# Forming one operand of the first stage on VectorE instead of by accumulating loads

## The chip, the cores and the metric

The kernel runs on one core of one Trainium2 chip. The metric is the time of one execution on the device in microseconds (us); the kernel before takes 1924.87 us (median of three runs, 1923.51 to 1925.85).

## The reference, cut to what matters

A two-layer decoder trunk on x of 1024 tokens by 1024 channels, in float32. Layer 0 begins with one wide projection of x, and this is the first stage of the kernel:

```
proj = x @ w_in                       # 1024 x 1024 by 1024 x (3*2048 + 8)
xm, o_pre, z, gts = split(proj, [E, 2*E, 3*E], axis=-1)      # E = 2048
```

From xm come a causal convolution and q, k and v of an mLSTM cell; o_pre and z gate its result; gts (8 columns) are the cell's input and forget gates. A layer norm, a gated embedding, a short-convolution layer and a second gated embedding follow.

## The kernel before, in words

All of it works on tiles of 128 partitions by 512 float32. x lies transposed: `raw_x[c, h]` is channel block c (0 to 7) of token half h (0 or 1). TensorE works on pairs: `split` (lines 86 to 94) makes of a tile a rounded part "hi" (a cast on ScalarE, L91) and the remainder "lo" (a subtraction on VectorE, L94), and `three` (L104, L105, L106) adds up hi by hi, hi by lo and lo by hi: three matmuls where one was. The third one needs the lo part of the weights.

The projection is a two-by-two block product done with seven block products instead of eight (class `Projection`). A group g is a pair of 128-column blocks of weights, with four weight tiles a11, a12 (first row) and a21, a22 (second row). Product (g, n) multiplies the n-th of a11, a12, s2, s1, s3, s4, a22, where the s are sums of weight tiles formed on VectorE (L118), by its partner n11, b21, t2, t1, n3, n22 or n4, which are four tiles each (k = 0 to 3) formed of x. Of these, in the code's signs:

- n3 = x(k, 1) - x(k+4, 1), t2 = x(k, 0) - n3: `moving_1`
- T1 = x(k, 1) - x(k, 0): `moving_t1n` and `moving_t1`
- n4 = x(k+4, 0) - t2: `moving_n4n` and `moving_n4`, formed by ScalarE (the negative, L123) and an accumulating load on POOL's queue (L135)

One product is 12 matmuls of 128 by 512. The first six groups go in two passes: products (0,0), (0,1), (1,0), ... (5,1) first, since they need token half 0 and the first weight rows alone, and then (0,2) to (0,6), (1,2) and so on. Weights are prepared three products ahead of their use.

The table `EARLY_OPERANDS` names, for each operand step, the product after which it is written in the code and how many k go with one product. The engines' streams are fixed when the program is built, and each engine works its stream in order. SP issues all plain loads in one queue of its own; each of them waits for the landing of the one eight places before it. POOL's queue carries the accumulating loads and the stores of results.

T1 is made in three steps before. After products 0 and 1 ScalarE writes -x(k, 0) into a new tile (L123, `moving_t1n`), POOL issues a load that adds x(k, 1) from HBM onto it (`add_on`, L135), and after products 7 and 8 the tile is split (`moving_t1`). `gpack`, whose gate weights VectorE turns into `wghl` after product 7 (`prepare_constants`), is loaded by SP behind the last tile of x. `cpack` holds the other constants.

Of the kernel before, what the change touches and what calls it, by code (L numbers as in the profile page):

```python
# [11 lines left out]
ALU = mybir.AluOpType  # L12

P = 128
HALF = 512
# [16 lines left out]
PACE = 0.85  # L32
STORE_AFTER = 8
GATES_AT = 32
EARLY_OPERANDS = (("t1n", 0, 2), ("t2", 1, 1), ("n22", 5, 2), ("n4n", 5, 2), ("n3", 6, 2), ("t1", 7, 2), ("n4", 10, 2), ("b12", 24, 1))
PLAN = {
    -10: [("head",)],
    -9: [("xc", 0)],
# [22 lines left out]
def trunk(ctx: ExitStack, tc: tile.TileContext, I, out: bass.AP):  # L61
# [9 lines left out]
    def slot(dt=F32):  # L71
        count[0] += 1
        return sl.tile([P, HALF], dt, tag="s", name=f"{part[0]}_{count[0]}")
# [14 lines left out]
    def split(src, hi_on, lo_on):  # L88
        hi, lo = slot(F32R), slot(F32R)
        if hi_on == "act":  # L90
            nc.scalar.copy(hi, src)  # L91
        else:
            nc.vector.tensor_copy(hi, src)
        (nc.vector if lo_on == "dve" else nc.gpsimd).tensor_tensor(  # L94
            out=lo, in0=src, in1=hi.bitcast(F32), op=ALU.subtract)
        return hi, lo

    def cols(j, n=P):
        return slice(j * n, (j + 1) * n)
# [16 lines left out]
    def combined(a, b, op):  # L116
        d = slot()
        nc.vector.tensor_tensor(out=d, in0=a, in1=b, op=op)  # L118
        return d

    def evacuated(src, scale=1.0):
        t = slot()
        nc.scalar.activation(t, src, AF.Copy, scale=scale)  # L123
        return t
# [8 lines left out]
    def add_on(dst, src):  # L133

        nc.gpsimd.dma_start(dst, src, accum_op=ALU.add)  # L135
# [311 lines left out]
    def operands():  # L447
        return {key: [None] * 4 for key in ("n11", "b21", "t2", "t1", "n3", "n22", "n4")}
# [7 lines left out]
    ops = operands()  # L456
    raw_x = {}

    def load_x(c, h):
        raw_x[c, h] = slot()  # L460
        nc.sync.dma_start(raw_x[c, h], I["xt"][cols(c), cols(h, HALF)])
# [39 lines left out]
    cell = Projection(groups, lambda i, j: WA[i, j], ops, cell_result, EARLY_A, LEAD_A)  # L501
# [35 lines left out]
    for k in range(4):  # L537
        load_x(k + 4, 1)
        load_x(k, 1)
        if k < 3:  # L540
            cell.fetch(k + 2, 1)
    nc.sync.dma_start(gpack, I["gpack"])
    nc.sync.dma_start(cpack, I["cpack"])

# [16 lines left out]
    b12 = [None] * 4  # L561

    def moving_1(k):
        n3 = combined(raw_x[k, 1], raw_x[k + 4, 1], ALU.subtract)
        raw_x["n3", k] = n3
        raw_x["t2", k] = combined(raw_x.pop((k, 0)), n3, ALU.subtract)
        ops["t2"][k] = split(raw_x["t2", k], "act", "dve")

    def moving_t1n(k):
        raw_x["t1", k] = evacuated(raw_x[k, 0], -1.0)  # L570
        add_on(raw_x["t1", k], I["xt"][cols(k), cols(1, HALF)])

    def moving_n4n(k):
        raw_x["n4", k] = evacuated(raw_x.pop(("t2", k)), -1.0)
        add_on(raw_x["n4", k], raw_x.pop((k + 4, 0)))

    def moving_t1(k):
        ops["t1"][k] = split(raw_x.pop(("t1", k)), "act", "dve")

    def moving_n3(k):  # L580
        ops["n3"][k] = split(raw_x.pop(("n3", k)), "act", "dve")
# [7 lines left out]
    def moving_b12(k):  # L589
        b12[k] = split(raw_x.pop((k, 1)), "act", "dve")  # L590

    moving = {"t1n": moving_t1n, "t2": moving_1, "n4n": moving_n4n, "t1": moving_t1, "n3": moving_n3,
              "n22": moving_n22, "n4": moving_n4, "b12": moving_b12}

    def transposed(blocks):
# [377 lines left out]
    early = {}  # L973
    for f, at, n in EARLY_OPERANDS:
        for k in range(4):
# [435 lines left out]
    ops = operands()  # L1411
# [218 lines left out]
def build(arrays):  # L1630
    import concourse.bacc as bacc

    nc = bacc.Bacc("TRN2", target_bir_lowering=False, num_devices=1)
    I = {k: nc.dram_tensor(k, v.shape, mybir.dt.from_np(v.dtype), kind="ExternalInput").ap()
         for k, v in arrays.items()}
    out = nc.dram_tensor("out", (DM, SEQ), F32, kind="ExternalOutput").ap()
    with tile.TileContext(nc) as tc:
        trunk(tc, I, out)
    return nc
# [9 lines left out]
```

## Time and profile before

| what | value |
|---|---|
| median of three runs | 1924.87 us |
| the profiled execution, own time | 1925.12 us |
| its span, first to last instruction | 1923.4 us |
| TensorE busy | 1896.8 us (99%) |
| VectorE busy | 1463.8 us (76%) |
| ScalarE busy | 937.8 us (49%) |
| mean granted TensorE clock | 0.997 |

Times below are us from the span's start. PE is TensorE, DVE is VectorE, ACT is ScalarE, SPq is SP's issuing of loads. In a row of the timeline the first number is the start, the second the length, and the bracket tells how long the engine had stood before it and what it waited for. Consecutive instructions of one engine overlap a little, so the distance of two starts, and not the length, is what one more instruction costs. Names with numbers left out ("in", "start", "xt") are those of tiles: "start" tiles are allocated ahead of the first product, "in" tiles behind it, "wa" are the weights and "xt" is x in HBM.

### The profile page before, as it was taken

How to read it: one execution, taken by the hardware profiler on the slowest of the kernel's cores; microseconds unless marked ns; L12 is line 12 of the kernel's file. 1: busy time of each engine (PE TensorE's matmuls, PEld its weight loads, DVE VectorE, ACT ScalarE, POOL GpSimd, SP SyncE). 2: the span in 40 equal slices, each digit the busy share in tenths (PEclk: the TensorE clock that was granted, in tenths of full speed). 3: DMA queues.
4: the chain of work that ended last, by engine and by line, in shares of the span. 5: the costliest groups of instructions: out<-in, count | busy, mean ns of one | idle time of the engine just before them, and what ended most of it. 6: DMA issues, size and time to landing. Idle time of an engine off the chain costs nothing.

```text
span 1923.4 us, 26056 instructions
## 1 busy us (share of the span) xinstructions
PE 1896.8 (99%) x8654; PEld 1563.6 (81%) x8654; DVE 1463.8 (76%) x2528; ACT 937.8 (49%) x1741; POOL 288.7 (15%) x344
## 2 busy tenths in 40 slices
PE   8999999999999999999999999999999999999998
PEld 6778888888888888787878888888888888888887
DVE  7888888778777777757977787878787877745657
ACT  7655554546656544455665433333333333454553
POOL 1112332222001000034301000000000000031420
PEclk9999999999999999999999999999999999999999
DMA  8247767686556584896135535545646355699435
GB/s 253 91 155 226 240 216 229 202 246 233 178 184 215 187 286 155 325 348 191 56 130 159 141 129 176 183 161 149 197 161 190 134 156 155 215 361 325 143 115 192
DMA packets 197400, 374.35 MB, mean 195 GB/s; under 512 B 22768, under 2 KB 27152, under 8 KB 197264
## 3 DMA queue, kind: packets, MB, share of 16 engines
q1 hardware_dynamic: 169008, 301.88, 45.5%
q0 software_dynamic: 28256, 70.80, 14.2%
q8 instruction: 68, 1.11, 0.2%
q14 instruction: 68, 0.56, 0.1%
HBM read 239.40 MB, written 115.36 MB: 184 GB/s over the span
## 4 chain that ended last, share of the span: by engine, by line
PE 86%; DVE 5%; DMA 3%; ACT 2%; issue 1%; POOL 1%; SPq 0%; DVEq 0%; POOLq 0%; ACTq 0%
PE Pb L106 11%; PE Pb L104 11%; PE Pb L105 11%; PE Pin L104 7%; PE Pin L106 7%; PE Pin L105 7%; PE Pat L104 3%; PE Pat L106 3%; PE Pat L105 3%; PE Poutb L105 3%; PE Poutb L104 3%; PE Poutb L106 3%; PE Pouta L105 2%; PE Pouta L106 2%; PE Pgb L104 2%; PE Pgb L106 2%
## 5 line engine op out<-in xcount | busy, mean ns | idle before, releaser
L104 PE MATMUL Pb<-ga,b 128*128 128x512 f32 x852 | 331.4, 389 | 0.0
L105 PE MATMUL Pb<-ga,b 128*128 128x512 f32 x852 | 331.4, 389 | 0.0
L106 PE MATMUL Pb<-ga,b 128*128 128x512 f32 x852 | 327.1, 389 | 0.0
L91 ACT CAST b<-b 128x512 fp32r<-128x512 f32 x265 | 152.5, 617 | 160.9 <-DVE b L118 158.6
L104 PE MATMUL Pin<-in,in 128*128 128x512 f32 x488 | 191.0, 391 | 2.4 <-ACT in L91 1.3
L105 PE MATMUL Pin<-in,in 128*128 128x512 f32 x488 | 190.0, 389 | 0.0
L94 DVE TENSOR_TENSOR b<-b,b 128x512 fp32r<-128x512 f32 x265 | 176.6, 687 | 17.0 <-ACT b L91 15.4
L106 PE MATMUL Pin<-in,in 128*128 128x512 f32 x488 | 189.0, 391 | 0.0
L106 PEld LDWEIGHTS Pb<-ga,b 128*128 128x128 f32 x852 | 159.9, 188 | 33.4 <-DVE b L94 0.2
L105 PEld LDWEIGHTS Pb<-ga,b 128*128 128x128 f32 x852 | 159.9, 188 | 33.3
L104 PEld LDWEIGHTS Pb<-ga,b 128*128 128x128 f32 x852 | 159.9, 188 | 33.1
L91 ACT CAST in<-in 128x512 fp32r<-128x512 f32 x175 | 105.5, 615 | 89.9 <-DVE in L118 78.4
L94 DVE TENSOR_TENSOR in<-in,in 128x512 fp32r<-128x512 f32 x175 | 118.6, 687 | 23.9 <-ACT in L91 23.2
L123 ACT ACTIVATE b<-Pb 128x512 f32<-128x512 f32 x96 | 57.4, 598 | 129.0 <-PE Pb L106 129.0
L104 PE MATMUL Pat<-at,at 128*128 128x512 f32 (+3 forms) x297 | 112.4, 379 | 0.9 <-ACT at L91 0.9
L118 DVE TENSOR_TENSOR b<-b,b 128x512 f32<-128x512 f32 x167 | 110.9, 687 | 1.0 <-issue 0.2
L106 PE MATMUL Pat<-at,at 128*128 128x512 f32 (+3 forms) x297 | 109.6, 372 | 1.2 <-DVE at L859 1.2
L104 PEld LDWEIGHTS Pin<-in,in 128*128 128x128 f32 x488 | 91.6, 188 | 23.4 <-ACT in L123 2.1
L105 PE MATMUL Pat<-at,at 128*128 128x512 f32 (+3 forms) x297 | 110.0, 371 | 0.0
L106 PEld LDWEIGHTS Pin<-in,in 128*128 128x128 f32 x488 | 91.6, 188 | 20.8 <-DVE in L94 1.7
L105 PEld LDWEIGHTS Pin<-in,in 128*128 128x128 f32 x488 | 91.6, 188 | 18.8
L94 DVE TENSOR_TENSOR outa<-outa,outa 128x512 fp32r<-128x512 f32 x108 | 77.0, 771 | 23.9 <-ACT outa L91 23.8
(424 smaller groups left out, 4230.5 us busy)
## 6 DMA issues: line engine op xcount, KB each, us to landing
b<-wb SPq DMA_DIRECT2D x122, 256.0 KB, 4.1
in<-wa SPq DMA_DIRECT2D x86, 256.0 KB, 4.1
xcdram<-in POOLq DMA_DIRECT2D x56, 256.0 KB, 4.6
ydram<-b SPq DMA_DIRECT2D x56, 256.0 KB, 2.1
gwdram<-b SPq DMA_DIRECT2D x56, 256.0 KB, 2.2
gb<-gwdram SPq DMA_DIRECT2D x56, 256.0 KB, 3.4
outa<-ydram SPq DMA_DIRECT2D x52, 256.0 KB, 5.4
outb<-ydram SPq DMA_DIRECT2D x49, 256.0 KB, 5.4
```

Source lines behind the costliest of these rows:

```text
L91: nc.scalar.copy(hi, src)
L94: (nc.vector if lo_on == "dve" else nc.gpsimd).tensor_tensor(out=lo, in0=src, in1=hi.bitcast(F32), op=ALU.subtract)
L104: mm(acc, lh, rh, start=first, stop=False, skip_group_check=onto)
L105: mm(acc, lh, rl, start=False, stop=False, skip_group_check=onto)
L106: mm(acc, ll, rh, start=False, stop=last, skip_group_check=onto)
L118: nc.vector.tensor_tensor(out=d, in0=a, in1=b, op=op)
L123: nc.scalar.activation(t, src, AF.Copy, scale=scale)
```

## The change

`moving_t1n` is gone, and with it four ScalarE instructions and four accumulating loads of 256 KB. x(k, 0) is kept until T1 is formed; `moving_t1`, at its old place after products 7 and 8, now subtracts the two tiles of x on VectorE (`combined`, L118) and splits the result. Two weight fetches are called ahead of the constants: the first weight row of group 5 and the second weight row of group 0.

```diff
-EARLY_OPERANDS = (("t1n", 0, 2), ("t2", 1, 1), ("n22", 5, 2), ("n4n", 5, 2), ("n3", 6, 2), ("t1", 7, 2), ("n4", 10, 2), ("b12", 24, 1))
+EARLY_OPERANDS = (("t2", 1, 1), ("n22", 5, 2), ("n4n", 5, 2), ("n3", 6, 2), ("t1", 7, 2), ("n4", 10, 2), ("b12", 24, 1))
...
         if k < 3:
             cell.fetch(k + 2, 1)
+    cell.fetch(5, 1)
+    cell.fetch(0, 2)
     nc.sync.dma_start(gpack, I["gpack"])
     nc.sync.dma_start(cpack, I["cpack"])
...
         raw_x["n3", k] = n3
-        raw_x["t2", k] = combined(raw_x.pop((k, 0)), n3, ALU.subtract)
+        raw_x["b11", k] = raw_x.pop((k, 0))
+        raw_x["t2", k] = combined(raw_x["b11", k], n3, ALU.subtract)
         ops["t2"][k] = split(raw_x["t2", k], "act", "dve")
-
-    def moving_t1n(k):
-        raw_x["t1", k] = evacuated(raw_x[k, 0], -1.0)
-        add_on(raw_x["t1", k], I["xt"][cols(k), cols(1, HALF)])
...
     def moving_t1(k):
-        ops["t1"][k] = split(raw_x.pop(("t1", k)), "act", "dve")
+        ops["t1"][k] = split(combined(raw_x[k, 1], raw_x.pop(("b11", k)), ALU.subtract), "act", "dve")
```

Nowhere else does an engine's stream change. On VectorE, from the lo part of T1 for k = 0 (in_454<-in_219 before) to the lo part of the weight sum s2 of product (0,2) and the sums behind it, the stream before reads:

```order
L94 TENSOR_TENSOR in_454<-in_219,in_453 128x512
L94 TENSOR_TENSOR in_458<-in_222,in_457 128x512
L94 TENSOR_TENSOR in_466<-in_340,in_465 128x512
L424 TENSOR_TENSOR in_482<-Pin_504,in_482 128x512
L94 TENSOR_TENSOR in_485<-in_243,in_484 128x512
L94 TENSOR_TENSOR in_489<-in_246,in_488 128x512
L118 TENSOR_TENSOR in_496<-in_461,in_463 128x512
L118 TENSOR_TENSOR in_498<-in_496,start_93 128x512
L94 TENSOR_TENSOR in_501<-in_498,in_500 128x512
```

and now, at the same place (in_447, in_453, in_478 and in_484 are the hi parts of T1 that ScalarE casts from the L118 results; start_161 and start_95 are x(0, 1) and x(0, 0); in_458<-start_189 is the lo part of the weights of product (5,1)):

```order
L118 TENSOR_TENSOR in_445<-start_161,start_95 128x512
L94 TENSOR_TENSOR in_448<-in_445,in_447 128x512
L118 TENSOR_TENSOR in_451<-start_169,start_97 128x512
L94 TENSOR_TENSOR in_454<-in_451,in_453 128x512
L94 TENSOR_TENSOR in_458<-start_189,in_457 128x512
L118 TENSOR_TENSOR in_476<-start_177,start_99 128x512
L424 TENSOR_TENSOR in_474<-Pin_500,in_474 128x512
L94 TENSOR_TENSOR in_479<-in_476,in_478 128x512
L118 TENSOR_TENSOR in_482<-start_185,start_101 128x512
L94 TENSOR_TENSOR in_485<-in_482,in_484 128x512
L118 TENSOR_TENSOR in_492<-start_191,start_193 128x512
L118 TENSOR_TENSOR in_494<-in_492,start_93 128x512
```

Each L94 of T1 now stands behind the L118 that forms its tile, for k = 0, 1 and 3 directly behind it.

On SP, from the last two tiles of x (start_183 and start_185 are x(7, 1) and x(3, 1)) on, the queue before reads:

```order
L461 DMA start_183<-xt 128x512
L461 DMA start_185<-xt 128x512
L542 DMA start_158<-gpack 128x192
L372 DMA in_338<-wa 128x512
L372 DMA in_340<-wa 128x512
L372 DMA in_418<-wa 128x512
L372 DMA in_420<-wa 128x512
```

and now:

```order
L461 DMA start_183<-xt 128x512
L461 DMA start_185<-xt 128x512
L372 DMA start_187<-wa 128x512
L372 DMA start_189<-wa 128x512
L372 DMA start_191<-wa 128x512
L372 DMA start_193<-wa 128x512
L544 DMA start_158<-gpack 128x192
```

`gpack` has moved behind four weight tiles; `cpack` stands far ahead of both pieces, at the same place in both kernels.

## Rows read from the trace of the kernel before

**Rows 1.** Busy time by window: window and its length, then busy us (instructions) of PE, PEld, DVE, ACT and POOL, granted clock, share of the DMA engines and GB/s.

```profile
60.00:160.00 100.00, 100.00 (x448) 78.52 (x447) 83.73 (x167) 55.95 (x97) 17.83 (x31) 1.00 0.42 137
160.00:300.00 140.00, 140.00 (x617) 115.34 (x616) 114.14 (x193) 78.84 (x138) 39.28 (x64) 1.00 0.76 238
```

**Rows 2.** TensorE's timeline: the first matmul of product (4,0), the last of (5,1), and the first of (0,2).

```profile
31.69 0.50 PE L104 MATMUL Pin<-start,in 128*128 128x512 f32 x1 [2.15 <-ACT in L91]
...
45.02 0.39 PE L106 MATMUL Pin<-start,in 128*128 128x512 f32 x1
46.70 0.50 PE L104 MATMUL Pin<-in,in 128*128 128x512 f32 x1 [1.29 <-ACT in L91]
```

**Rows 3.** Timeline of VectorE and ScalarE before the first of these waits ends: the lo part of weights, the first L118 for k = 3 (it reads x(3, 1) and x(7, 1)), the second L118 (t2), the lo part of t2; and ScalarE's cast of the weights of (4,0).

```profile
25.62 0.69 DVE L94 TENSOR_TENSOR in<-start,in 128x512 fp32r<-128x512 f32 x1
28.57 0.69 DVE L118 TENSOR_TENSOR in<-start,start 128x512 f32<-128x512 f32 x1 [2.26 <-DMA start<-xt]
...
29.78 0.68 DVE L118 TENSOR_TENSOR in<-start,in 128x512 f32<-128x512 f32 x1
31.15 0.69 DVE L94 TENSOR_TENSOR in<-in,in 128x512 fp32r<-128x512 f32 x1 [0.68 <-ACT in L91]
...
31.02 0.61 ACT L91 CAST in<-start 128x512 fp32r<-128x512 f32 x1
```

**Rows 4.** SP's timeline: the issue of the last tile of x, x(3, 1), and of `gpack` behind it.

```profile
17.06 0.33 SPq L461 DMA_DIRECT2D start<-xt  x1
17.74 0.33 SPq L542 DMA_DIRECT2D start<-gpack  x1
```

**Rows 5.** Loads issued from 7 to 15 us: issues, KB each, median us from issue to landing.

```profile
start<-xt SPq DMA_DIRECT2D x6, 256.0 KB, 5.3
```

**Rows 6.** The same from 15 to 31 us, with the share of POOL's queue (packets, MB, share of 16 engines' time).

```profile
q0 software_dynamic: 656, 1.31, 39.6%
...
in<-xt POOLq DMA_DIRECT2D x4, 256.0 KB, 9.0
...
start<-xt SPq DMA_DIRECT2D x2, 256.0 KB, 10.7
```

**Rows 7.** Timeline of VectorE and ScalarE: L118 forms t2 for k = 0, ScalarE casts it, VectorE takes its lo part.

```profile
17.01 0.69 DVE L118 TENSOR_TENSOR in<-start,in 128x512 f32<-128x512 f32 x1
...
18.39 0.69 DVE L94 TENSOR_TENSOR in<-in,in 128x512 fp32r<-128x512 f32 x1 [0.69 <-ACT in L91]
...
17.74 0.62 ACT L91 CAST in<-in 128x512 fp32r<-128x512 f32 x1 [1.03 <-DVE in L118]
```

**Rows 8.** Timeline of VectorE and ScalarE from 37 to 47 us. The eight L94 are n3 (k = 0, 1), the weights of (5,0), n3 (k = 2, 3), T1 (k = 0, 1) and the weights of (5,1); the two that follow are L424 in between and T1 for k = 2, 3; then the sums of group 0, and ScalarE's cast and VectorE's lo part of s2.

```profile
37.88 4.91 DVE L94 TENSOR_TENSOR in<-in,in 128x512 fp32r<-128x512 f32 x8
...
43.31 1.28 DVE L94 TENSOR_TENSOR in<-in,in 128x512 fp32r<-128x512 f32 x2
44.51 0.68 DVE L118 TENSOR_TENSOR in<-in,in 128x512 f32<-128x512 f32 x1
45.23 0.69 DVE L118 TENSOR_TENSOR in<-in,start 128x512 f32<-128x512 f32 x1
46.68 0.69 DVE L94 TENSOR_TENSOR in<-in,in 128x512 fp32r<-128x512 f32 x1 [0.76 <-ACT in L91]
...
37.24 4.26 ACT L91 CAST in<-in 128x512 fp32r<-128x512 f32 x8
...
46.03 1.14 ACT L91 CAST in<-in 128x512 fp32r<-128x512 f32 x2 [1.97 <-DVE in L118]
```

**Rows 9.** TensorE's timeline: the third matmul of (5,0) and the third of (5,1), the first ones that need the lo part of their weights.

```profile
39.83 0.50 PE L106 MATMUL Pin<-start,in 128*128 128x512 f32 x1
...
42.85 0.50 PE L106 MATMUL Pin<-start,in 128*128 128x512 f32 x1
```

**Rows 10.** TensorE's timeline: the matmuls that end two other waits of this run.

```profile
632.78 1.49 PE L815 MATMUL Pat<-at,at 128*128 128x128 f32 x11 [1.54 <-DVE at L917]
...
789.70 0.50 PE L105 MATMUL Pouta<-outa,outa 128*128 128x512 f32 x1 [1.75 <-DVE outa L129]
```

**Rows 11.** Busy time by window (columns as in rows 1) behind the waits of rows 2 and 10; the granted clock stands third from the end.

```profile
33.60:36.60 3.00, 3.00 (x9) 2.32 (x8) 3.00 (x6) 3.00 (x7) 2.05 (x4) 0.50 0.78 257
...
634.00:636.00 2.00, 2.00 (x14) 1.78 (x13) 2.00 (x5) 1.79 (x5) 0.00 (x0) 1.00 0.20 75
792.00:794.00 2.00, 2.00 (x6) 1.58 (x5) 2.00 (x5) 1.85 (x4) 0.00 (x0) 0.50 0.13 50
...
47.00:50.00 3.00, 3.00 (x13) 2.13 (x12) 3.00 (x6) 2.40 (x6) 0.00 (x0) 1.00 0.00 0
```

**Rows 12.** TensorE's timeline: the first matmul of the slow stretch behind the first wait, and the first after it; eight start in between, the first one included.

```profile
33.55 0.63 PE L104 MATMUL Pin<-start,in 128*128 128x512 f32 x1
...
36.94 0.40 PE L106 MATMUL Pin<-start,in 128*128 128x512 f32 x1
```

**Rows 13.** VectorE reads the bank of (0,4) (L434); TensorE's last matmul of (0,5) and its first of (0,6), which adds onto that bank.

```profile
57.64 0.69 DVE L434 TENSOR_TENSOR in<-Pin,in 128x512 f32<-128x512 f32 x1
...
57.91 0.39 PE L106 MATMUL Pin<-in,in 128*128 128x512 f32 x1
58.38 0.50 PE L104 MATMUL Pin<-in,in 128*128 128x512 f32 x1
```

**Rows 14.** VectorE's timeline: the first instruction that reads `gpack`.

```profile
36.60 0.19 DVE L556 CAST wghl<-start 128x64 fp32r<-128x64 f32 x1
```

More of the change, by code (lines that the diff above doesn't have):

```diff
@@ L590, in moving_b12 @@
         b12[k] = split(raw_x.pop((k, 1)), "act", "dve")
-    moving = {"t1n": moving_t1n, "t2": moving_1, "n4n": moving_n4n, "t1": moving_t1, "n3": moving_n3,
+    moving = {"t2": moving_1, "n4n": moving_n4n, "t1": moving_t1, "n3": moving_n3,
               "n22": moving_n22, "n4": moving_n4, "b12": moving_b12}
```

## Prediction, made before the changed kernel ran

> **What bounds the kernel now.** I read the table first: TensorE is busy 99% of the span, so only what makes it wait can move the end. The windows then say where: from 60 to 300 us it is busy in every microsecond [rows 1], so what it loses before 60 is carried to the end, and what it gains there too. The first 60 us hold two waits of TensorE [rows 2]: 2.15 us ahead of product (4,0), 1.29 us ahead of (0,2). Both are laid to ScalarE's casts, so the next view is what ScalarE and VectorE did. Ahead of the first, VectorE had stood 2.26 us for tiles of x for k = 3 [rows 3]; ScalarE's cast of the weights of (4,0), at 31.02, stands in line behind the cast of t2, which needs these tiles. The last of them was issued at 17.06 [rows 4] and used at 28.57: more than 11 us, where the loads issued from 7 to 15 us took 5.3 [rows 5]. The accumulating loads on POOL's queue ran in between, took 9.0 us each, and with one store their queue held 39.6% of the DMA engines' time [rows 6]. Ahead of (0,2) it is another thing: VectorE has no room. From 37.88 its rows follow each other without a gap until the sums of group 0 [rows 8], and TensorE waits for the cast of s2 at their end. The third matmuls of (5,0) and (5,1), the first to need the lo part of their weights, come at 39.83 and 42.85 [rows 9]; the lo parts are the third and the eighth of the row of eight and end at 37.88 + 2 x 0.603 + 0.69 = 39.78 and at 42.79 [rows 8]: TensorE goes at VectorE's pace there.
>
> **The change, part by part.** Times are those of the profiled execution (1925.12 us, 0.25 above the median); I add the difference to the median.
>
> *No accumulating loads.* Without them the last tile of x should take about what its like took earlier, 5.3 us, plus some for the one store left on POOL's queue: it would land near 23. VectorE ends what stands ahead at 25.62 and the next start is 0.60 later (eight starts in rows 8: (4.91 - 0.69) / 7 = 0.603), so its first L118 for k = 3 comes at 26.22 instead of 28.57. **Gain 2.35 us**, and not more, since the chain ahead (t2 for k = 0 to 2, each a way from VectorE to ScalarE and back) doesn't depend on the loads; it needs only that the tile takes under 26.22 - 17.06 = 9.2 us. The bounds are 0 and 2.35. The first wait of TensorE goes with it. ScalarE's four instructions that go cost nothing now: ScalarE stood 1.03 us for VectorE right behind them [rows 7].
>
> *Four subtractions on VectorE.* They stand in the stretch that has no gap, between the lo part of n3 and the sums: 4 x 0.603 = **2.41 us** (bounds 2.41 and 4 x 0.69 = 2.76).
>
> *The new waits.* VectorE now writes a tile, ScalarE casts it, and the very next instruction on VectorE takes the lo part, so VectorE stands, and everything queued behind: the next T1, the weights of (5,1), L424, the sums of group 0, the lo part of s2. What such a way costs is to be seen where t2 is made: 17.01 to 18.39, 1.38 us from start to start [rows 7], in place of 0.60. That is 0.78 for k = 0, 1 and 3; for k = 2 L424 stands between, 1.38 - 2 x 0.60 = 0.17. Together **2.51 us** (bounds: 0, if all were covered, and 4 x 0.78 = 3.12; the rows give the middle). Before, T1 lay ready and no such wait was there.
>
> *gpack behind four weight tiles.* Issues follow 0.68 apart [rows 4], so it goes out near 20.5 and lands by 31.2 even at the slow 10.7 us [rows 6]; its first reader comes at 36.60 - 2.35 = 34.25 [rows 14]. Nothing; if it came late, VectorE would stand for the difference. The four weight tiles are needed after 35 and go out near 18 to 20: nothing either. cpack doesn't move.
>
> *At s2.* -2.35 + 2.41 + 2.51 = +2.57: the lo part of s2 at 49.25 instead of 46.68, the first matmul of (0,2) at 49.3 instead of 46.70. TensorE waited there for just this, so it is late by the whole sum, and from there on both streams stand as before. TensorE has nothing later to catch up in before 300 us.
>
> *TensorE's clock.* The waits of TensorE change place. (5,0)'s third matmul comes 2.35 earlier, at 37.5; (5,1) waits for two T1 first, -2.35 + 2 x (0.60 + 0.78) = +0.41: third matmul at 43.3. A matmul takes 140.00 / 617 = 0.227 us where TensorE doesn't wait [rows 1], so twelve later, at 40.2, it would be ready for that one: 3 us are waited in front of it, most ahead of the product's first matmul. (5,1) then ends 0.41 later than before and (0,2) starts 2.57 later: 1.29 + 2.57 - 0.41 = 3.45 us of waiting. Behind the wait of 2.15 us the granted clock was 0.50, that is 1.2 GHz in place of 2.4, and behind 1.75 us too; behind 1.54 and 1.29 us it stayed at 1.00 [rows 2, 10, 11]. A wait longer than any of these makes the low clock likely. Its price: eight matmuls took 36.94 - 33.55 = 3.39 us in place of 8 x 0.227 = 1.82 [rows 12], 1.57 us. That stretch cost nothing before, since VectorE was late there. Now it would fall on (0,2) and (0,3), where TensorE sets the pace, less the wait ahead of (0,6), 58.38 - 57.91 - 0.23 = 0.24 [rows 13], which it swallows. Bounds 0 and 1.57; part of it may lie inside the wait, so I take 0.9, between the half and the whole.
>
> [...]
>
> **The sum.** +2.57 + 0.9 = +3.5 us: 1924.87 + 3.5 = 1928.4 us. This kernel's time can be told from no change from about 0.2%, 3.85 us, on; so I forecast a loss on the edge of what shows.
>
> **The rivals.**
> - *The clock stays up.* +2.57 alone: 1927.4. For it: behind the waits of 1.54 and 1.29 us it stayed up [rows 2, 10, 11]. Against: none was as long as 3.45.
> - *Slower: the low clock falls wholly on (0,2) and (0,3).* It decides when the slow stretch begins only after 49.3, as the one before began 1.9 us after its wait [rows 2, 12]. Then 2.57 + 1.57 = +4.1, 1929.0, and 1930 if a second stretch follows. [...]
> - *VectorE has the room after all.* If the four waits lie in time that VectorE would have stood anyway, 2.41 - 2.35 is left: 1924.9. Against: rows 8 show no such time.
> - *Faster: the loads were all.* If the late tile alone set the stage, TensorE loses neither 2.15 nor 1.57 nor 1.29: -5.0, 1919.9. For it: the first wait is just that. Against: the second isn't, and the change makes VectorE's stream longer just there.
>
> **How the numbers follow.** Forecast 0.40, clock up 0.18, slower 0.22, room 0.12, faster 0.08. Of the forecast's 0.40 some 0.06 lies over 3.85 us, as do the 0.22: slower 0.28. Faster is the last rival, 0.08. The rest is within 0.2%: 0.64. For 8 in 10 the range leaves out the faster rival, the lower edge of the room case and the tail beyond two slow stretches: 1924.3 to 1929.8.
>
> **What would show it.** Right: the first L118 for k = 3 near 26.2 with no wait for a load, and no 2 us wait ahead of (4,0); three waits of VectorE of 0.7 to 0.8 us for ScalarE's L91 between 38 and 47 us; TensorE waiting about 2 us ahead of (5,1) and about 3.4 ahead of (0,2), which begins near 49.3; a clock of 0.50 in some window from 50 to 54; everything from 60 us on shifted by one amount. Wrong: T1's L94 following its L118 without a wait; (0,2) at or before 46.7; or the tile of x still landing after 26.2, which would take the gain and make the loss 5 us.

## The result and the profile after

The changed kernel takes 1929.85 us (median of 13 runs) beside 1924.87 us for the kernel before (13 runs of its own): a ratio of 1.0025, 95% interval 1.0018 to 1.0032. That is 5.0 us slower; forecast were 3.5, with 1928.4 us and a range up to 1929.8. The profiled execution after has a span of 1928.9 us, 5.5 us more than the one before.

First the loads. The view is that of the DMA transfers from 15 to 31 us: the share of POOL's queue (packets, MB, share of 16 engines' time) and the issues by tile (KB each, median us to landing).

```profile
q0 software_dynamic: 80, 0.26, 4.1%
...
start<-xt SPq DMA_DIRECT2D x2, 256.0 KB, 6.0
```

POOL's queue held 39.6% there before, and the same tiles of x took 10.7 us [rows 6]. What the early tile did is in VectorE's timeline, and so is what took the gain away:

```profile
25.90 0.69 DVE L94 TENSOR_TENSOR in<-start,in 128x512 fp32r<-128x512 f32 x1
26.50 0.69 DVE L118 TENSOR_TENSOR in<-start,start 128x512 f32<-128x512 f32 x1
...
38.82 0.68 DVE L118 TENSOR_TENSOR in<-start,start 128x512 f32<-128x512 f32 x1
40.24 0.69 DVE L94 TENSOR_TENSOR in<-in,in 128x512 fp32r<-128x512 f32 x1 [0.74 <-ACT in L91]
40.85 0.68 DVE L118 TENSOR_TENSOR in<-start,start 128x512 f32<-128x512 f32 x1
42.27 0.69 DVE L94 TENSOR_TENSOR in<-in,in 128x512 fp32r<-128x512 f32 x1 [0.74 <-ACT in L91]
...
43.49 0.69 DVE L118 TENSOR_TENSOR in<-start,start 128x512 f32<-128x512 f32 x1
...
44.87 0.69 DVE L94 TENSOR_TENSOR in<-in,in 128x512 fp32r<-128x512 f32 x1
45.47 0.68 DVE L118 TENSOR_TENSOR in<-start,start 128x512 f32<-128x512 f32 x1
46.90 0.69 DVE L94 TENSOR_TENSOR in<-in,in 128x512 fp32r<-128x512 f32 x1 [0.74 <-ACT in L91]
...
49.65 0.69 DVE L94 TENSOR_TENSOR in<-in,in 128x512 fp32r<-128x512 f32 x1 [0.74 <-ACT in L91]
```

The first subtraction for k = 3 (26.50) follows the lo part ahead of it (25.90) by 0.60 us, with no wait for a load; before, these were 28.57 and 25.62, with 2.26 us of standing between them [rows 3]. From 38.82 on each T1 is formed (L118), cast by ScalarE, and VectorE stands 0.74 us ahead of its lo part, three times. For k = 2 (43.49 and 44.87) L424 stands in between and the bracket is missing. The last row is the lo part of s2, at 49.65, where it was 46.68 [rows 8].

TensorE's timeline has the waits in the brackets; then the windows around the last one (busy time and count by engine, and third from the end the granted clock):

```profile
36.86 0.50 PE L104 MATMUL Pin<-start,in 128*128 128x512 f32 x1 [0.84 <-ACT in L91]
...
42.81 0.50 PE L104 MATMUL Pin<-start,in 128*128 128x512 f32 x1 [2.50 <-ACT in L91]
...
49.67 0.80 PE L104 MATMUL Pin<-in,in 128*128 128x512 f32 x1 [3.49 <-ACT in L91]
50.27 0.63 PE L105 MATMUL Pin<-in,in 128*128 128x512 f32 x1
...
54.96 0.42 PE L104 MATMUL Pin<-in,in 128*128 128x512 f32 x1
```

```profile
43.00:46.00 3.00, 2.92 (x12) 1.91 (x11) 2.91 (x5) 1.50 (x3) 0.00 (x0) 1.00 0.00 0
...
48.30:49.60 1.30, 0.00 (x0) 0.00 (x0) 0.61 (x1) 0.60 (x2) 0.00 (x0) 0.50 0.00 0
...
50.40:54.80 4.40, 4.40 (x12) 3.53 (x11) 4.40 (x8) 3.80 (x8) 0.00 (x0) 0.50 0.00 0
55.00:58.00 3.00, 3.00 (x15) 2.44 (x14) 3.00 (x6) 1.15 (x3) 0.58 (x1) 1.00 0.57 179
```

The wait of 2.15 us ahead of (4,0) [rows 2] is gone. In its place stand 0.84 us ahead of (5,0), 2.50 ahead of (5,1) and 3.49 ahead of (0,2). Behind the 2.50 us the clock stayed at 1.00. In the longest wait it fell: it was 0.50 (1.2 GHz in place of 2.4) from 48.30 to 49.60 already, while TensorE still stood, and then on: from 50.27 to 54.96 eleven matmuls start, 4.69 us where 11 x 0.227 = 2.50 would do. That is 2.19 us lost. From 60 to 300 us TensorE is busy in every microsecond, as before [rows 1]:

```profile
60.00:160.00 100.00, 100.00 (x448) 79.00 (x446) 82.98 (x166) 55.63 (x96) 16.93 (x30) 1.00 0.39 130
160.00:300.00 140.00, 140.00 (x617) 115.08 (x616) 116.27 (x198) 78.90 (x139) 40.64 (x66) 1.00 0.77 236
```

So what stood at 60 us is carried on. The first wait of TensorE behind 60 us is one of 1.05 us for ScalarE's L123, and the matmul behind it is a good milestone (called M below): it starts at 323.51 us before and at 328.02 after.

```profile
323.51 0.50 PE L104 MATMUL Pin<-in,in 128*128 128x512 f32 x1 [1.05 <-ACT in L123]
```

```profile
328.02 0.50 PE L104 MATMUL Pin<-in,in 128*128 128x512 f32 x1 [1.06 <-ACT in L123]
```

4.51 us are there by then. Further on the distance of the two executions goes with half-clock stretches that the one has and the other has not (last section): 4.20 us at the wait near 790, 2.53 at the next one near 825, 4.22 near 1010. From there it grows in small steps to 5.23 at the last matmul; what makes these is not shown.

### The profile page after: what moved, and what is told of

Its sections match the earlier page's. It is cut to its first block, busy times and chain, and to the rows that moved or that the text cites. A ratio compares the mean times of both kernels' runs of the same rounds, so it can differ in the third digit from the quotient of the medians.

```text
span 1928.9 us, 26042 instructions
## 1 busy us (share of the span) xinstructions
PE 1898.8 (98%) x8654; PEld 1564.5 (81%) x8654; DVE 1468.3 (76%) x2532; ACT 936.7 (49%) x1737; POOL 282.9 (15%) x340
## 4 chain that ended last, share of the span: by engine, by line
PE 85%; DVE 6%; DMA 4%; ACT 3%; issue 2%; POOL 1%; SPq 0%; DVEq 0%; ACTq 0%; POOLq 0%
PE Pb L106 11%; PE Pb L105 11%; PE Pb L104 11%; PE Pin L104 7%; PE Pin L106 7%; PE Pin L105 7%; PE Pat L104 3%; PE Pat L106 3%; PE Pat L105 3%; PE Poutb L105 3%; PE Poutb L104 3%; PE Poutb L106 3%; DMA outa<-ydram 1%; PE Pga L104 1%; PE Pgb L106 1%
## 5 line engine op out<-in xcount | busy, mean ns | idle before, releaser
L94 DVE TENSOR_TENSOR b<-b,b 128x512 fp32r<-128x512 f32 x265 | 176.3, 684 | 18.0 <-ACT b L91 16.4
L94 DVE TENSOR_TENSOR in<-in,in 128x512 fp32r<-128x512 f32 x172 | 117.0, 686 | 26.1 <-ACT in L91 25.2
L123 ACT ACTIVATE b<-Pb 128x512 f32<-128x512 f32 x96 | 57.4, 598 | 128.2 <-PE Pb L106 128.1
L118 DVE TENSOR_TENSOR b<-b,b 128x512 f32<-128x512 f32 x167 | 110.6, 685 | 0.8
L94 DVE TENSOR_TENSOR outa<-outa,outa 128x512 fp32r<-128x512 f32 x108 | 78.9, 785 | 24.8 <-ACT outa L91 24.6
```

Source lines behind the costliest of these rows:

```text
L94: (nc.vector if lo_on == "dve" else nc.gpsimd).tensor_tensor(out=lo, in0=src, in1=hi.bitcast(F32), op=ALU.subtract)
```

## The experiments

The theory is the prediction's: VectorE's stream ahead of s2 sets the start of (0,2). The early tile of x shortens it, the four subtractions and the ways over ScalarE (VectorE writes a tile, ScalarE casts it, VectorE takes the lo part) lengthen it, and the long wait of TensorE then brings a half clock. The rivals: the new order of SyncE's loads; that only the waits, or only the instructions, or only the clock cost.

Executions differ by up to 1.3 us in when the same early instructions start (25.62 to 26.87 in the column "lo part"). So the table has a distance inside one execution: from VectorE's lo part ahead of its first subtraction for k = 3 (25.62 before, 25.90 after; in the early-T1 kernel from 25.74, the 26.34 of its row less the 0.60 of the subtraction that now stands ahead) to the first matmul of (0,2). Beside it stands M, which has in it all that follows up to 322 us, and also how late the execution started: of e7's 7.81 us 1.25 are its later lo part, and e9 would be 2.52 ahead without its own 0.52.

| kernel | lo part | (0,2) | distance | against before | M against before | ratio of times, 95% interval |
|---|---|---|---|---|---|---|
| before | 25.62 | 46.70 | 21.08 | | | |
| e9: no T1 at all | 26.14 | 44.84 | 18.70 | -2.38 | -2.00 | 0.9985 (0.9976 to 0.9993) |
| e4: T1 formed ahead | 25.82 | 46.92 | 21.10 | +0.02 | +0.09 | 1.0003 (0.9995 to 1.0012) |
| after | 25.90 | 49.67 | 23.77 | +2.69 | +4.51 | 1.0025 (1.0018 to 1.0032) |
| e1: T1 part alone | 25.77 | 49.48 | 23.71 | +2.63 | +4.65 | 1.0022 (1.0013 to 1.0032) |
| e7: T1 formed twice | 26.87 | 53.13 | 26.26 | +5.18 | +7.81 | 1.0032 (1.0019 to 1.0045) |
| e2: order of loads alone | 26.07 | 46.88 | 20.81 | -0.27 | +0.06 | 0.9999 (0.9991 to 1.0008) |
| e3: T1 formed early | 25.74 | 45.04 | 19.30 | -1.78 | -1.82 | 0.9987 (0.9979 to 0.9996) |

**Which part of the change: e1 and e2.** e1 is the changed kernel without the two lines that put gpack behind four weight tiles; e2 is the kernel before with these two lines alone:

```
+    cell.fetch(5, 1)
+    cell.fetch(0, 2)
     nc.sync.dma_start(gpack, I["gpack"])
```

> The changed kernel with its first part alone: T1 by VectorE, no accumulating loads; gpack stays at its old place ahead of the four weight tiles. Theory (VectorE's longer stream makes the loss): all of it is kept, product (0,2) begins near 49.5 us and the time is that of the changed kernel, +5 us, ratio near 1.0025 to the kernel before. Rival (the order of SyncE's loads makes the loss): the loss goes, 1924 to 1926 us, ratio near 1.000.

> The kernel before with the second part alone: gpack behind four weight tiles, accumulating loads as before. Theory: nothing moves, product (0,2) near 46.7 us, the wait of VectorE for the tile of x for k = 3 stays near 2.3 us, 1924 to 1926 us, ratio 1.000. Rival (the order of the loads makes the loss): about +5 us, ratio near 1.0025.

Measured: 1928.66 and 1924.03 us beside 1924.94 for the kernel before. TensorE's row at (0,2), of e1 and of e2:

```profile
49.48 0.79 PE L104 MATMUL Pin<-in,in 128*128 128x512 f32 x1 [3.48 <-ACT in L91]
```

```profile
46.88 0.50 PE L104 MATMUL Pin<-in,in 128*128 128x512 f32 x1 [1.30 <-ACT in L91]
```

The loss is T1's; the order of the loads alone shows no loss. The 0.27 us of e2's distance are the tile of x, for which VectorE stood 2.00 us there in place of 2.26.

**One term at a time: e9, e4, e7.** e9 leaves T1's subtraction out (the plain tile of x is split in its place): the removal of the loads alone. e4 forms T1 one product before it is split, so that the four instructions stay in the full stretch but no lo part follows its own subtraction. e7 makes each subtraction twice.

```
 e9   ops["t1"][k] = split(raw_x.pop(("b11", k)), "act", "dve")
 e4   EARLY_OPERANDS: ... ("n3", 6, 2), ("t1s", 6, 2), ("t1", 7, 2) ...
      t1s:  raw_x["t1", k] = combined(raw_x[k, 1], raw_x.pop(("b11", k)), ALU.subtract)
      t1:   ops["t1"][k] = split(raw_x.pop(("t1", k)), "act", "dve")
 e7   combined(raw_x[k, 1], raw_x["b11", k], ALU.subtract)      # added ahead of T1's own line
```

> The changed kernel without the four subtractions: T1 is not formed, and the plain tile of x stands in its place, so that part of the computation is left out. What remains is the removal of the accumulating loads alone. Theory (the early tile of x passes through whole): VectorE's first subtraction for k = 3 near 26.3 us, no wait of 0.74 us for T1, product (0,2) near 44.5 us, 2.35 us faster than the kernel before, 1922.5 us, ratio 0.9988. Rival (the early tile gives nothing at the end, and the loss of the change is its own): ratio 1.000.

> The changed kernel, with the four subtractions formed one product earlier than their tiles are split, so that they stand in the same full stretch of VectorE, but no lo part follows its own subtraction at once. It takes the round trips away and keeps the instructions. Theory: of +2.57 us at (0,2) the +2.41 - 2.35 = +0.06 is left, (0,2) near 46.8 us (47.1 with the later start of that execution) and no wait of 0.74 us on VectorE between 38 and 50 us; the wait of TensorE ahead of (0,2) is some 2.7 us, so a low clock may follow it: +0.1 us without it, +1.6 with it, ratio 1.0000 to 1.0009. Rival (the instructions cost the loss, not the waits): (0,2) near 49 us, ratio 1.0025.

> The changed kernel with each subtraction of T1 made twice, the first into a tile that nobody reads: four more instructions in the same place. Theory (every instruction there passes through whole): (0,2) 4 x 0.603 = 2.41 us later than in the changed kernel, near 52.1 us, and TensorE waits longer for it, so that the half clock behind it stays: 2.4 us slower than the changed kernel, near 1932.3 us, ratio 1.0038 to the kernel before. Rival (VectorE has room there, and the loss is the clock's or the round trips'): ratio 1.0025.

Measured: 1921.38 us beside 1924.98, 1924.83 beside 1924.94, 1931.05 beside 1924.55 (five runs of e7). The table's distances make a ladder: -2.38 without T1, +0.02 with the instructions (a step of 2.40), +2.69 with the ways over ScalarE too (a step of 2.67), +5.18 with the instructions once more (2.49). In e4 VectorE runs through where it stood three times in the changed kernel:

```profile
39.94 1.28 DVE L118 TENSOR_TENSOR in<-start,start 128x512 f32<-128x512 f32 x2
41.15 1.28 DVE L94 TENSOR_TENSOR in<-in,in 128x512 fp32r<-128x512 f32 x2
42.35 0.68 DVE L94 TENSOR_TENSOR in<-start,in 128x512 fp32r<-128x512 f32 x1
...
46.90 0.69 DVE L94 TENSOR_TENSOR in<-in,in 128x512 fp32r<-128x512 f32 x1 [0.74 <-ACT in L91]
```

The one wait left is s2's own, which the kernel before has too; the expectation had overlooked it. It was also wrong on TensorE: the 2.7 us of waiting did not come in one piece ahead of (0,2) but as 1.36 us inside (5,0) and 1.27 ahead of (0,2), and the clock at (0,2) stayed up. A half clock did come, behind the 1.36 us (0.50 from 38.60 to 41.80), but it ended before (0,2) and nothing of it is seen at M (+0.09). So the waits of VectorE alone, the instructions alone and the removed loads alone are each refuted as the whole cause, and each is a part.

**The clock: e5.** Fourteen matmuls on a tile of zeros, into the bank that (0,3) starts afresh, stand ahead of (0,2) in the changed kernel (the trace has records of 13):

```
+    if n == 2 and (g, n) == (0, 2):
+        s.b2 = bank()
+        for _ in range(14):
+            mm(s.b2, warm[:, :P], warm, start=True, stop=True)
```

> The changed kernel with 14 matmuls on a tile of zeros, into a bank that (0,3) writes afresh, put into TensorE's wait of 3.48 us ahead of product (0,2); 14 x 0.227 = 3.2 us fit into it. Theory (the wait brings the half clock, and it costs what was left over after the forecast's 0.9): (0,2) still near 49.7 us, but no half clock from 50 to 55 us; the 2.2 us of that stretch go, about 1927.6 us, ratio 1.0014 to the kernel before. Rival (the half clock behind the wait costs nothing, as the one at 33 us before): ratio 1.0025, 1929.8 us. Rival (the half clock comes from something else, and comes here too): 1.0025, with the slow matmuls still there.

Measured: 1928.33 us beside 1924.55, ratio 1.0016 (1.0007 to 1.0025).

```profile
43.62 0.63 PE L105 MATMUL Pin<-start,in 128*128 128x512 f32 x1
...
47.41 3.20 PE L414 MATMUL Pin<-warm 128*128 128x512 bf16 x13
50.26 0.58 PE L104 MATMUL Pin<-in,in 128*128 128x512 f32 x1
```

```profile
50.40:54.80 4.40, 4.40 (x21) 3.60 (x21) 4.40 (x9) 3.80 (x8) 0.00 (x0) 1.00 0.00 0
```

In this execution the half clock came a product earlier, behind the 2.50 us ahead of (5,1) (the 0.63 rows), so that the filling began late and (0,2) started at 50.26, 0.4 us behind its s2. Yet the clock from 50.4 to 54.8 was 1.00, and M is 3.02 us behind the kernel before instead of 4.51: the half clock on (0,2) is worth about 1.5 us there, or 1.7 with the executions' own starts taken off. The other traces say the same. From the first matmul of (0,2) to M it is 276.65 to 276.81 us in the seven with a full clock behind (0,2) (before, e2, e3, e4, e6, e8, e9), and 278.19 to 278.68 in the three with a half clock (after, e1, e7). The medians of e5 and of the changed kernel lean the same way, but their intervals overlap.

**Where else T1 could be formed: e3, e8, e6.** e3 forms T1 where t2 is made, between t2's subtraction and the lo part for which VectorE waits 0.69 us anyway. e8 does so on GpSimd. e6 is the kernel before with the accumulating loads three products later.

```
 e3   raw_x["t2", k] = combined(raw_x[k, 0], n3, ALU.subtract)
     +raw_x["t1", k] = combined(raw_x[k, 1], raw_x.pop((k, 0)), ALU.subtract)
      ops["t2"][k] = split(raw_x["t2", k], "act", "dve")
 e8  +nc.gpsimd.tensor_tensor(out=raw_x["t1", k], in0=raw_x[k, 1], in1=raw_x.pop((k, 0)), op=ALU.subtract)
 e6   EARLY_OPERANDS: ("t1n", 0, 2), ("t2", 1, 1) -> ("t2", 1, 1), ("t1n", 3, 2)
```

> The changed kernel, with the four subtractions of T1 moved forward to where t2 is made: each stands between t2's own subtraction and the lo part that waits 0.69 us for ScalarE. Theory: three of the four lie in that wait, the one for k = 1 (where another instruction stands there already) costs 0.6 us; the round trips between 38 and 50 us go; of the tile that lands early 2.35 - 0.6 = 1.75 us is left: product (0,2) near 45 us, no low clock from 50 to 55 us, 1.7 us faster than the kernel before, 1923 us, ratio 0.999, and near 6.7 us faster than the changed kernel. Rival (what counts is VectorE's busy time wherever it stands): -2.35 + 2.41, ratio 1.000. Rival (the loads or the weights make the loss): ratio 1.0025.

> The third experiment (T1 formed early, where t2 is made) with the four subtractions on GpSimd in place of VectorE. Theory (VectorE's row decides): VectorE loses the 0.6 us that the one for k = 1 cost it, (0,2) near 44.5 us, 0.6 us faster than that kernel, ratio 0.9985 to the kernel before. Rival (GpSimd disturbs VectorE while it works): VectorE's instructions from 17 to 32 us last longer than 0.69 us, (0,2) later than 45.0 us, ratio 0.999 or more.

> The kernel before, with the accumulating loads of T1 issued three products later, behind the last tile of x in time; nothing is added to VectorE. It does the removal's good alone. Theory (the tile of x lands early by 2.35 us and VectorE's row is as before): no wait of VectorE for a load at 26 to 28 us, product (0,2) near 44.5 us, 2.35 us faster than the kernel before, 1922.5 us, ratio 0.9988. Rival (the accumulating loads now land too late: issued near 26 and 30 us, at 9 us they land near 35 and 39, ScalarE wants the tiles from 37.5 us on): ScalarE waits for them and (0,2) stays at or behind 46.7 us, ratio 1.000 or more. Rival (the gain of the early tile does not reach the end): 1.000 without such a wait.

Measured: e3 1922.06 us beside 1924.94; e8 1927.82 beside 1924.55, ratio 1.0014 (1.0005 to 1.0023); e6 1924.53 beside 1924.55, ratio 0.9998 (0.9989 to 1.0007). e3 went as expected: the fourth subtraction lies in the wait, whose bracket is gone:

```profile
28.15 0.68 DVE L118 TENSOR_TENSOR in<-start,in 128x512 f32<-128x512 f32 x1
28.75 0.69 DVE L118 TENSOR_TENSOR in<-start,start 128x512 f32<-128x512 f32 x1
29.52 0.69 DVE L94 TENSOR_TENSOR in<-in,in 128x512 fp32r<-128x512 f32 x1
```

It is the same arithmetic as the change, 0.38% faster by the two ratios, and faster than both kernels. In e8 the rival holds, GpSimd first and VectorE behind it:

```profile
15.88 1.32 POOL L570 TENSOR_TENSOR in<-start,start 128x512 f32<-128x512 f32 x1
17.45 1.45 POOL L570 TENSOR_TENSOR in<-start,start 128x512 f32<-128x512 f32 x1 [0.25 <-DMA start<-xt]
```

```profile
16.04 1.72 DVE L94 TENSOR_TENSOR in<-start,in 128x512 fp32r<-128x512 f32 x1 [1.34 <-ACT in L91]
17.68 1.77 DVE L118 TENSOR_TENSOR in<-start,start 128x512 f32<-128x512 f32 x1
```

Four instructions of VectorE that start while GpSimd works last 1.67 to 1.77 us in place of 0.69, and each ends 0.55 us or a little more after GpSimd's: 17.76 and 17.20, 19.45 and 18.90. VectorE waited until GpSimd was through. (0,2) comes at 49.99. In e6 neither theory nor rival was right: the tile of x did land early and T1 was ready in time, but the two negatives that ScalarE makes ahead of the loads (L123) now stand in front of a cast for which VectorE waits:

```profile
25.12 1.15 ACT L123 ACTIVATE in<-start 128x512 f32<-128x512 f32 x2
26.18 0.60 ACT L91 CAST in<-start 128x512 fp32r<-128x512 f32 x1
```

```profile
26.81 0.69 DVE L94 TENSOR_TENSOR in<-start,in 128x512 fp32r<-128x512 f32 x1 [0.87 <-ACT in L91]
```

The same again at 31.55 (0.86 us). The two take most of what the early tile gave, and (0,2) is at 46.58.

**Can more be had: e10, e11.** e10 is e3 with the four splits of T1 moved behind that of s2 (`("t1", 7, 2)` -> `("t1", 9, 4)`); e11 also puts the subtraction for k = 1 between s2's sum and its lo part.

> The third experiment (T1 formed early), with the four splits of T1 moved behind the split of s2, which needs nothing of T1; T1 is first read by (0,3). Theory (VectorE's row ahead of s2 is the limit): s2's lo part 2.4 us earlier than in that kernel, near 42.6 us, where TensorE is still busy with (5,1) until near 43.8; its wait of 1.24 us ahead of (0,2) goes, 1.2 us faster than that kernel, 1920.8 us, ratio 0.998 to the kernel before. Rival (the four splits are then missing ahead of (0,3), where VectorE is as full): TensorE waits in or ahead of (0,3) for about what it saved, ratio 0.9987 as that kernel.

> The kernel of experiment e10 with the subtraction for k = 1 put into the wait of 0.74 us between s2's sum and its lo part, where VectorE stands idle for ScalarE, instead of at t2, where it cost 0.6 us. Theory: all four subtractions now lie in waits of VectorE, everything from 23 us on is 0.6 us earlier than in e10, 1920.2 us, ratio 0.9977 to the kernel before. Rival (VectorE is the limit behind (0,2) in e10 already): the instruction is paid there and nothing changes against e10.

Measured: 1922.70 us, ratio 0.9995 (0.9987 to 1.0004), and 1922.60, 0.9996 (0.9988 to 1.0005), beside 1924.98. In e10 the wait ahead of (0,2) is gone and two others stand behind it:

```profile
47.70 0.50 PE L106 MATMUL Pin<-in,in 128*128 128x512 f32 x1 [0.87 <-DVE in L94]
51.00 0.50 PE L104 MATMUL Pin<-in,in 128*128 128x512 f32 x1 [0.74 <-ACT in L123]
```

M is 1.66 us ahead of the kernel before, e3's is 1.82: the rival holds, VectorE is as full behind (0,2). In e11 M is 2.53 us ahead, which speaks against the rival named there, but the time doesn't show it; between 322 and 630 us its profiled execution lost 2.1 us more than e3's. Whether e11 is worth more than e3 stays open; of the kernels that compute T1, e3 alone is shown to be faster than the kernel before.

## Why the prediction was right, and where it was short

Direction, path and order of size were right; the time is 1.5 us above the forecast, at the range's upper end and 0.05 us beyond it.

- *No accumulating loads*, -2.35: right. e9 has -2.38 alone.
- *Four subtractions*, +2.41: right. e4 against e9 has 2.40, and e7 has 2.49 for four more.
- *Ways over ScalarE*, +2.51: 2.67 (after against e4). There were three waits of 0.74 us, as forecast, but each way took 1.42 us from start to start (38.82 to 40.24) where 1.38 had been counted; the fourth, where L424 stands between, took its 1.38 (43.49 to 44.87).
- *gpack*, 0: right (e2 shows no change in M or in the time).
- *At s2*, +2.57: measured +2.69 by the distance. The waits of TensorE, 2.50 and 3.49 us, had been put at about 2 and 3.45.
- *TensorE's clock*, +0.9: the step that was short. The length of the slow stretch was taken over from the one that rows 12 show, eight matmuls in 3.39 us, less what lay in the wait. A part did lie in the wait (0.50 from 48.30 to 49.60), but the stretch was about twice as long: it reached to 54.96, and eleven matmuls started in it behind the first of (0,2), thirteen in e1 and ten in e7. They cost 2.19 us. Of these, M shows 4.51 - 2.97 = 1.54; some 0.65 was taken back in small waits that TensorE has behind (0,2) before and not after, where 0.24 had been counted. e5 shows the same 1.5 from the other side. Why the stretch was longer here than behind the wait of 2.15 us stays open.

With 1.54 in place of 0.9 and 2.69 in place of 2.57 the sum is 4.2 us, 1929.1. The rival that had the low clock wholly on (0,2) and (0,3) gave 1929.0, but that it comes so near is luck: its stretch was one of eight matmuls that began only behind the wait. The ratio's interval, 3.5 to 6.2 us, holds it. The last microsecond is not settled: the median lies 0.8 us above, less than executions differ by.

The Trainium skill (TensorE: Matmul & The Clock Gate, section HAM oscillation — how this bites in real kernels) says that a wait between groups of matmuls throttles TensorE once it is long enough, and that the next group then starts cold. In these traces that held behind every wait of 3.48 to 3.74 us in the first stage (after, e1, and both waits of e7), behind one of three of 2.45 to 2.50 (e5, not after or e1), and behind none of 1.24 to 1.30 ahead of (0,2). In between, the length does not decide (last section).

## What to carry to other kernels

Taking a transfer off the queue is worth only the time until the next thing is late, and work that replaces it has to be placed, not only costed: the same four subtractions cost 5 us in a full stretch of VectorE, directly ahead of the cast and the subtraction that use them, and 0.6 us (e3 against e9) in waits that were there anyway. Where a tile goes from VectorE to ScalarE and back, put another VectorE instruction between. And when a wait of the busiest engine grows, count what follows it too: here 1.5 us of clock came on top.

## What the runs showed of the hardware that was not expected

- GpSimd as a helper for VectorE costs more than it brings here: a subtraction of two tiles on GpSimd took 1.32 to 1.72 us, and VectorE's two-input instruction started meanwhile did not end before it. The Trainium skill (SBUF — State Buffer, section Who interferes with whom) has this: a VectorE instruction with two inputs in SBUF contends with a GpSimd instruction that reads SBUF, and the later one is blocked and not slowed. The rows of e8 agree.
- The half clock is not a fixed answer to a wait's length. It came behind 1.36 us in e4 and not behind 2.03 us in e8, both in the first stage:

```profile
38.88 0.80 PE L106 MATMUL Pin<-start,in 128*128 128x512 f32 x1 [1.36 <-DVE in L94]
...
38.60:41.80 3.20, 2.92 (x7) 2.37 (x8) 3.20 (x7) 2.42 (x5) 0.00 (x0) 0.50 1.08 287
```

```profile
27.89 0.50 PE L104 MATMUL Pin<-start,in 128*128 128x512 f32 x1 [2.03 <-ACT in L91]
...
28.00:30.00 2.00, 1.92 (x8) 1.28 (x9) 1.93 (x4) 0.00 (x0) 0.00 (x0) 1.00 0.03 8
```

At one place it can come in one execution and not in another. Behind the wait of 1.75 us near 790 us it was 0.50 in the execution before [rows 11], and after, behind 1.75 us too, it is 1.00. Behind a wait near 970 us (1.88 us before, 1.87 after) it is the other way round, 0.50 after and not before; the two windows are of the changed kernel:

```profile
794.50:797.00 2.50, 2.50 (x13) 2.06 (x12) 2.50 (x5) 1.49 (x3) 0.00 (x0) 1.00 0.42 165
973.40:976.00 2.60, 2.60 (x8) 2.03 (x7) 1.51 (x4) 2.48 (x5) 0.90 (x1) 0.50 0.58 197
```

- Such stretches shift a single execution: each of these two moved the distance of before and after by some 1.65 us (4.20 to 2.53, and 2.59 to 4.22). e9's profile has none behind its waits, and its span is 6.3 us under that of the kernel before, where its median is 3.6 us under.
